# Two-layer attention encoder on one core: source order kept longer, returned outputs split a step ahead, more early subtractions on GpSimd

## The chip, the cores and the metric

The kernel runs on one core of a Trainium2 chip. A core has a matrix engine (TensorE, PE in the profile; its weight loads are listed as PEld), a vector engine (VectorE, DVE), a scalar engine (ScalarE, ACT), a general engine (GpSimd, POOL) and a queue engine that issues most transfers (SyncE, SP). Each engine works through its own list of instructions in order and waits at an instruction until what it needs is there. The metric is the device time of one execution in microseconds.

## The reference

Input x has 512 tokens of width 1024, in float32. Two layers follow one another, each with the same frame: RMS norm, one projection to queries, keys, values and a gate, attention with RMS-normed queries and keys, output times silu(gate), output projection, residual add.

```python
def mixer_a(hn, w_in, w_out, q_gain, k_gain, t5_bias):      # layer A
    qkv = proj[..., :n_qkv].reshape(b, s, N_DIL_GROUPS, 3, N_HEADS, HEAD_DIM)
    for g, (window, dilation) in enumerate(((128, 1), (512, 4), (2048, 16))):
        q = rms_norm(qkv[:, :, g, 0], q_gain[g]); k = rms_norm(qkv[:, :, g, 1], k_gain[g])
        o, lse = dilated_group_attention(q, k, qkv[:, :, g, 2], ..., dilation, reach)
        ...
    y = jnp.sum(softmax(lses)[..., None] * outs, axis=0) * jax.nn.silu(gate)
    return y @ w_out
```

Layer A is dilated sliding-window attention with three dilations (1, 4, 16), 16 heads each, merged by their softmax denominators. Layer B is neighbourhood attention on an 8 x 64 grid with 16 heads.

## The kernel before

**Products.** All products are in float32 accuracy made of three passes in a faster format: a weight block `wraw` is cast to `wh` on ACT (`cast`, line 157), the rest `wl = wraw - wh` is subtracted on DVE or POOL (`rest`, line 162), and PE multiplies high by high, high by low and low by high (`mm3`). A job is one 512 (or 384) columns wide block of weights: one cast, one subtraction, then its matmuls. `splits` (line 292) makes the jobs four to five ahead of PE, and chooses the engine of each subtraction by a fraction `pool[0] = [a, b]`: a of b subtractions go to POOL.

**Layer A.** The heads are taken in eight pairs (`hc` = 0 to 7). `main_a` is PE's main work for a pair: the projections. For pairs 1 to 7 it uses a scheme with seven block products in place of eight, on sums of weight blocks and on sums `mixed` of halves of the normed input. These four sums are made once, in `mix` (line 525), and split into `mix_h` (cast on ACT) and `mix_l` (subtracted on POOL or DVE). `gate_a` projects the gate, `v0_a` the values of the first dilation. `attn_a` works on the pair before, woven into the projections: `q_a` and `k_a` transpose queries and keys on PE into PSUM banks (`tp`) and copy them out (`k0h`, `k0l`, `q0h`, `q0l`, `q12`, `k12`), `scores` makes logits (`log`), `minima`, `exponents` and `normalise` make the softmax, the probabilities are transposed into `pt`, and `weigh` makes the products with v (`o`). `head_norm` scales raw queries and keys (`rawq`, `rawk`) by the inverse root `rs` of their sums of squares `ss`; the root is a chain of eleven tiny DVE instructions on `nv`, `na` and `rs`. Four PSUM banks hold accumulators (`acc`), four hold everything else.

**Between the layers.** The outputs of pairs 0 to 5 go to DRAM (`y_d`). At the end of layer A `y_back` brings them back into a tile `yr`, and `y_split` splits each into `y_h` (ACT) and `y_l` (DVE for odd pairs, POOL for even ones). Pair 6 is split straight from its tile `gt`. `out_product` then runs the output projection over `y_h` and `y_l`, first four output blocks for pair 0, then pair 1 and so on, while the attention of pair 7 is woven in; the products with pair 7 come last.

**What sets the order.** PE's list is the order of the source, in which `run` weaves the attention and all timed calls (`later_on`) into the projections by a clock that counts PE's own work. The lists of the other engines are made by a scheduler, which may move an instruction, unless it is marked: while `held[0]` is true every instruction of DVE, ACT, POOL and SP that is written through `vec`, `act`, `pol` and `syn` is kept in the order of the source. `main` sets `held[0] = hc > 0` at the start of each pair, and `project_qk`'s `normed` sets it false once the keys of pair 7 are scaled.

Of the kernel before, what the change touches and what calls it, by code (L numbers as in the profile page):

```python
# [13 lines left out]
F32 = mybir.dt.float32  # L14
# [8 lines left out]
P = 128  # L23
S = 512
D = 1024
DH = 64
NHC = 8
# [19 lines left out]
def tile_hybrid_encoder(  # L47
# [244 lines left out]
    def splits():  # L292
        casts, queue, due = [], [], plan.loads(lead)
        for at, (raw, c, step, n) in enumerate(plan.jobs):
            pool[0] = [0, 1] if at < start_jobs + 16 else [1, 2] if at < mixed_jobs else [2, 5]
            for r in due.get(at, ()):
                load(r)
            for add in plan.sums.get(at, ()):
                add()
            casts.append((cast(raw.tile[:, c : c + step], step), n))  # L300
            if len(casts) > 1:
                done, m = casts.pop(0)
                queue.append((*rest(*done), m))
            if len(queue) > 4:
                yield queue.pop(0)
        done, m = casts.pop(0)
        queue.append((*rest(*done), m))
        yield from queue
# [216 lines left out]
    def mix():  # L525


        x11, x12, x21, x22 = (x_all[:, k : k + KH, t : t + H] for t in (0, H) for k in (0, KH))
        t = wk.tile([P, 2, KH, H], F32, tag="tr", name="mixed", bufs=1)
        a, b = t[:, 0], t[:, 1]  # L530

        def put(n, out, op, x, y, eng):
            with in_order():
                op(out, x, y)
                act.copy(mix_h[:, n], out)
                eng.tensor_sub(mix_l[:, n], out, mix_h[:, n].bitcast(F32))
            stamp["mix", n] = 0

        yield "wait", ("first",), 500
        yield from first_out()  # L540
        yield 1500
        put(0, a, vec.tensor_sub, x21, x22, pol)
        yield 2000
        put(1, b, vec.tensor_sub, a, x11, vec)
        yield 2000
        yield from bias_lines()
        yield "wait", ("rawk", 0), 1000
        put(3, b, vec.tensor_add, b, x12, pol)
        yield 5000
        put(2, a, vec.tensor_sub, x11, x21, vec)  # L550

    def row_sums(ssq):

# [38 lines left out]
    st = {}  # L592
# [19 lines left out]
    def project_qk(n, ns, key, hc, guard, first=False, **kw):  # L612
# [3 lines left out]
        def evac(i, acc):  # L616
            if not box:
                box.append(raw_q() if key == "rawq" else part(0) if key == "rawk" else raw_b(hc, n))
                box.append(sums())
            raw, ss = box  # L620
            dst, src = raw[:, i, :], acc[:, :n]
            if first:
                act.copy(dst, src)
                return
            act.activation(dst, src, AF.Copy, scale=rs_n[:, i : i + 1])
            (squares_soon if key != "raw" else squares)(raw[:, i, : ns * 64], ss, i, ns, key != "raw")
# [10 lines left out]
    def normed(raw, ss, ns, key, hc):  # L637

        def go():
            with in_order() if hc == 0 and key != "raw" else nullcontext():  # L640
                head_norm(raw, ss, ns, key == "raw")
            st[key, hc] = raw
            stamp[key, hc] = clock[0]
            if (key, hc) == ("rawk", NHC - 1):
                held[0] = False

        if (key, hc) == ("rawk", 0):
            later_on(4000, go)
# [24 lines left out]
    def v0_a(hc, guard=None):  # L673
        acc = []
        yield from project_t(acc)
        yield guard
        home = "q12" if hc < NHC - 1 else "tr"
        vt = wk.tile([P, 1024], F32, tag=home, name="vt", bufs=1)
        act.copy(by_place(vt[:, 64:EXT]), by_class(acc[0]))
        act.copy(vt[:, 0:64], vt[:, EXT - 64 : EXT])  # L680
        st["vt", hc] = vt
# [177 lines left out]
        return gt  # L859

    def y_back(hcs, tag):
        t = wk.tile([P, 4, S], F32, tag=tag, name="yr", bufs=1)
        syn.dma_start(t[:, : len(hcs), :], y_d[:, hcs[0] : hcs[-1] + 1, :])
        return t

    def y_split(t, hc):
        src = t.rearrange("p (t ja x) -> p x ja t", t=4, ja=8)
# [70 lines left out]
    def attn_a(hc):  # L938
# [122 lines left out]

        if last:
            rows = []
            for u in range(2):
                room = part(0)
                mine = [
                    (tile_[:2], *minima(*tile_, room[:, n, :] if u else None)) for n, tile_ in enumerate(scores(u))
                ]
                for _, _, row, mn in mine:
                    exponents(row, mn)  # L1070
                    normalise(row, mn)
                rows += mine
                yield 4000
            for (hd, t), pr, _, _ in rows:
                turn_p(hd, t, pr)
                yield 700
            yield from v_a(hc)
            yield "wait", ("gate", hc), 500
            gt = weighed(hc, (yield from weigh()))
            stamp["ya", "turned"] = 0  # L1080
            for c in range(4):
                src = gt.rearrange("p (t ja x) -> p x ja t", t=4, ja=8)[:, 4 * c : 4 * c + 4]
# [33 lines left out]
        if hc < NHC - 2:  # L1116
# [7 lines left out]
                yield 1500  # L1124
                yield from q_a(hc + 1)
            return
        back = y_back(range(4), "tr")
        stamp["back",] = 0
        yield "wait", ("rawk", hc + 1), 0
        for n in range(2):  # L1130
            y_split(back[:, n, :], n)
        for n in (2, 3):
            later_on(3000 + 2000 * n, partial(y_split, back[:, n, :], n))
        yield from q_a(hc + 1)
        more = y_back(range(4, NHC - 2), "rawq")
        for n in range(4, NHC - 2):
            later_on(2000 * n - 3000, partial(y_split, more[:, n - 4, :], n))
        later_on(9000, partial(y_split, gt, hc))

    pending = []  # L1140

# [378 lines left out]
```

## Time and profile before

| | |
|---|---|
| median of the runs | 864.33 us (861.68 to 864.4) |
| the profiled execution | 865.5 us, of which the span of instructions is 863.7 us |
| PE busy | 838.7 us (97%) |
| DVE, ACT, POOL busy | 630.8, 509.1, 288.7 us |
| mean granted PE clock | 0.988 of full speed |
| subtractions `wl` | 207 on DVE, 153 on POOL |

Layer A's projections run from about 2 to 523 us, its output projection to about 600 us, layer B to the end. The figures in the profile are microseconds from the start of the span unless marked ns; a bracket at the end of a row of the timeline is how long the engine sat idle before the row, and what ended the wait. In tables by stretch, PEclk is the clock granted to PE (1.00 is full speed).

### The profile page before, as it was taken

The page shows a single profiled execution, that of the slowest core. Times are in us where ns is not written, and L with a number is a line of the kernel's source. Part 1 is how long each engine was busy: PE and PEld are TensorE (multiplying, and loading weights), DVE is VectorE, ACT ScalarE, POOL GpSimd, SP SyncE. Part 2 cuts the span into 40 slices and gives each one's busy share as a digit, 9 for nine tenths or more (in the row PEclk, how much of TensorE's full clock was granted, in tenths as well). Part 3 has the DMA queues.
Part 4 walks back from the last instruction along what each step waited for, and adds up shares of the span by engine and source line. Part 5 has one row for each costly group of instructions (what it writes and reads, how often), then busy time and mean ns, then how long its engine had stood idle before and what let it go on. Part 6 is the DMA issues. An engine that isn't in the chain of part 4 may idle for free. (4 is left out here: it accounts for less than half of the span.)

```text
span 863.7 us, 18127 instructions
## 1 busy us (share of the span) xinstructions
PE 838.7 (97%) x6611; PEld 693.6 (80%) x6611; DVE 630.8 (73%) x1655; ACT 509.1 (59%) x1066; POOL 288.7 (33%) x257
## 2 busy tenths in 40 slices
PE   9989988999999999999999998999999999999998
PEld 6867767878877878878878876889998898889776
DVE  6889894787887787887787866547577667866742
ACT  7565763674765855946846828545366645665440
POOL 5041531363462452442543513111223223322301
PEclk9999998999999999999999998999999999999999
DMA  9424755567667765775776662284264456545212
GB/s 341 131 62 125 192 125 146 107 164 216 128 164 216 147 165 176 153 181 166 162 172 182 137 217 104 74 275 139 93 173 143 125 166 184 162 129 139 83 50 98
DMA packets 56169, 131.97 MB, mean 153 GB/s; under 512 B 7184, under 2 KB 24528, under 8 KB 55952
## 3 DMA queue, kind: packets, MB, share of 16 engines
q1 hardware_dynamic: 49744, 108.78, 40.8%
q0 software_dynamic: 6048, 22.02, 15.0%
q8 instruction: 52, 0.85, 0.4%
q14 instruction: 37, 0.30, 0.1%
q10 hardware_dynamic: 288, 0.01, 0.0%
HBM read 111.73 MB, written 11.72 MB: 143 GB/s over the span
## 5 line engine op out<-in xcount | busy, mean ns | idle before, releaser
L85 POOL TENSOR_TENSOR wl<-wraw,wh 128x512 fp32r<-128x512 f32 (+1 forms) x153 | 197.8, 1294 | 448.5 <-PE acc L323 227.8
L85 ACT CAST wh<-wraw 128x512 fp32r<-128x512 f32 (+1 forms) x360 | 209.9, 593 | 194.3 <-PE acc L323 152.7
L85 DVE TENSOR_TENSOR wl<-wraw,wh 128x512 fp32r<-128x512 f32 (+1 forms) x207 | 160.4, 779 | 49.3 <-PE acc L323 34.5
L323 PE MATMUL acc<-wh,hn_h 128*128 128x384 f32 (+1 forms) x488 | 186.7, 382 | 3.1 <-DVE gt L85 1.8
L323 PE MATMUL acc<-wl,hn_h 128*128 128x384 f32 (+1 forms) x488 | 178.2, 365 | 2.7 <-DVE wl L85 2.7
L323 PE MATMUL acc<-wh,hn_l 128*128 128x384 f32 (+1 forms) x488 | 178.0, 365 | 0.0
L85 ACT ACTIVATE p<-p,mn 128x256 f32<-128x256 f32 (+2 forms) x248 | 137.8, 584 | 33.8 <-DVE mn L85 33.8
L323 PEld LDWEIGHTS acc<-wh,hn_h 128*128 128x128 f32 x488 | 92.5, 189 | 21.8 <-issue 6.6
L323 PEld LDWEIGHTS acc<-wl,hn_h 128*128 128x128 f32 x488 | 92.8, 190 | 11.2 <-DVE wl L85 3.7
L323 PEld LDWEIGHTS acc<-wh,hn_l 128*128 128x128 f32 x488 | 92.4, 189 | 9.9
L323 PE MATMUL acc<-wl,mix_h 128*128 128x512 f32 x224 | 87.4, 390 | 1.9 <-DVE wl L85 1.5
L323 PE MATMUL acc<-wh,mix_h 128*128 128x512 f32 x224 | 89.1, 398 | 0.0
L323 PE MATMUL acc<-wh,mix_l 128*128 128x512 f32 x224 | 87.4, 390 | 0.0
L323 PE MATMUL acc<-hn_h,wh 128*128 128x512 f32 x192 | 79.3, 413 | 0.3 <-ACT rawb L85 0.2
L323 PE MATMUL acc<-hn_h,wl 128*128 128x512 f32 x192 | 75.7, 394 | 3.1 <-DVE wl L85 3.1
L323 PE MATMUL acc<-hn_l,wh 128*128 128x512 f32 x192 | 75.7, 394 | 0.0
L85 DVE STREAM_TRANSPOSE pt<-p 128x512 f32<-128x512 f32 (+1 forms) x60 | 40.6, 688 | 23.8 <-ACT p L85 23.6
L85 DVE TENSOR_REDUCE ss<-sq 128x4 f32<-128x256 f32 (+1 forms) x96 | 46.3, 502 | 13.6 <-ACT sq L85 6.8
L323 PE MATMUL acc<-y_h,wh 128*128 128x512 f32 x128 | 52.6, 411 | 2.5 <-ACT gt L85 1.9
L323 PEld LDWEIGHTS acc<-wl,mix_h 128*128 128x128 f32 x224 | 42.1, 188 | 11.0 <-DVE wl L85 2.0
L323 PE MATMUL acc<-y_l,wh 128*128 128x512 f32 x128 | 50.4, 394 | 0.0
L323 PE MATMUL acc<-y_h,wl 128*128 128x512 f32 x128 | 50.3, 393 | 0.0
(145 smaller groups left out, 1364.1 us busy)
## 6 DMA issues: line engine op xcount, KB each, us to landing
wraw<-in_w SPq DMA_DIRECT2D x95, 512.0 KB
wraw<-in_w POOLq DMA_DIRECT2D x42, 512.0 KB, 7.0
wraw<-in_w SPq DMA_DIRECT2D x38, 384.0 KB
pt<-pt SPq DMA_DIRECT2D x112, 64.0 KB
td<-tr SPq DMA_DIRECT2D x24, 224.0 KB
pt<-td SPq DMA_DIRECT2D x24, 224.0 KB
e<-l_d SPq DMA_DIRECT2D x32, 112.0 KB
e<-l_d SPq DMA_DIRECT2D x16, 128.0 KB
```

Source lines behind the costliest of these rows:

```text
L85: m = f(*args, **kw)
L323: nc.tensor.matmul(o, l, r, **kw)
```

## The change

Five edits. (1) `held[0]` becomes true when the first keys of pair 0 are taken out of PSUM, earlier than before, and stays true until the last products with v (`weigh` of pair 7) are written. Where the last pair's softmax was a plain list of instructions, it now comes by timed calls, as that of the other pairs. (2) The `mix_l` of the mixed sum n = 2, the last of the four to be made, goes from DVE to POOL. (3) For the 24 jobs that follow the first 32, two of three subtractions go to POOL, where it was one of two: 16 instead of 12. (4) `y_back` brings pairs 0 and 1 first and then pairs 2 to 5 in one transfer, where it was 0 to 3 and then 4 and 5; the split of pair n is called at 1000 + 2500 n of the clock after the second transfer's call, that of pair 6 at 16000. (5) The last pair's `vt` (raw values) is put into the free half of the first `yr` tile, where it had to wait for a tile that held returned outputs.

```diff
@@ splits
-            pool[0] = [0, 1] if at < start_jobs + 16 else [1, 2] if at < mixed_jobs else [2, 5]
+            first = at - start_jobs
+            pool[0] = [0, 1] if first < 16 else [2, 3] if first < 40 else [1, 2] if at < mixed_jobs else [2, 5]
@@ mix
-        put(2, a, vec.tensor_sub, x11, x21, vec)
+        put(2, a, vec.tensor_sub, x11, x21, pol)
@@ project_qk
+                held[0] = held[0] or (key == "rawk" and hc == 0)
...
-            if (key, hc) == ("rawk", NHC - 1):
-                held[0] = False
@@ v0_a
-        home = "q12" if hc < NHC - 1 else "tr"
-        vt = wk.tile([P, 1024], F32, tag=home, name="vt", bufs=1)
+        vt = st["tail"][:, 1024:] if hc == NHC - 1 else wk.tile([P, 1024], F32, tag="q12", name="vt", bufs=1)
@@ y_back
-        t = wk.tile([P, 4, S], F32, tag=tag, name="yr", bufs=1)
-        syn.dma_start(t[:, : len(hcs), :], y_d[:, hcs[0] : hcs[-1] + 1, :])
-        return t
+        t = wk.tile([P, 4 * S], F32, tag=tag, name="yr", bufs=1)
+        y = t[:, : len(hcs) * S].rearrange("p (n s) -> p n s", n=len(hcs))
+        syn.dma_start(y, y_d[:, hcs[0] : hcs[-1] + 1, :])
+        return t, y
@@ attn_a, last pair
+            def soft(n, tile_, room):
+                pr, row, mn = minima(*tile_, room)
+                rows.append((*tile_[:2], pr))
+                later_on(1500, partial(exponents, row, mn))
+                later_on(2900, partial(normalise, row, mn))
+
             for u in range(2):
                 room = part(0)
-                mine = [
-                    (tile_[:2], *minima(*tile_, room[:, n, :] if u else None)) for n, tile_ in enumerate(scores(u))
-                ]
-                for _, _, row, mn in mine:
-                    exponents(row, mn)
-                    normalise(row, mn)
-                rows += mine
-                yield 4000
-            for (hd, t), pr, _, _ in rows:
-                turn_p(hd, t, pr)
+                for n, tile_ in enumerate(scores(u)):
+                    later_on(400 + 900 * n, partial(soft, n, tile_, room[:, n, :] if u else None))
+                yield 5000
+            for n in range(8):
+                turn_p(*rows[n])
                 yield 700
             yield from v_a(hc)
             yield "wait", ("gate", hc), 500
             gt = weighed(hc, (yield from weigh()))
+            held[0] = False
@@ attn_a, pair 6
-        back = y_back(range(4), "tr")
+        st["tail"], back = y_back(range(2), "tr")
...
-        for n in (2, 3):
-            later_on(3000 + 2000 * n, partial(y_split, back[:, n, :], n))
         yield from q_a(hc + 1)
-        more = y_back(range(4, NHC - 2), "rawq")
-        for n in range(4, NHC - 2):
-            later_on(2000 * n - 3000, partial(y_split, more[:, n - 4, :], n))
-        later_on(9000, partial(y_split, gt, hc))
+        _, more = y_back(range(2, NHC - 2), "rawq")
+        for n in range(2, NHC - 2):
+            later_on(1000 + 2500 * n, partial(y_split, more[:, n - 2, :], n))
+        later_on(16000, partial(y_split, gt, hc))
```

Most lists stay as they were. PE's own list is the same up to the first logits of the last pair. The other lists differ at three places. In the rows below, the number behind a name counts tiles; the same tile can have another number in the two kernels.

DVE at the end of the first keys' projection (pair 0) and the start of pair 1, before; `wl_617` belongs to the first half of gate 0:

```order
L85 TENSOR_TENSOR hn_l_93<-pt_98,hn_h_92 128x512
L85 TENSOR_TENSOR mix_l_95<-mixed_401,mix_h_94 128x1024
L85 TENSOR_REDUCE ss_582<-sq_584 128x4
L85 TENSOR_REDUCE ss_582<-sq_591 128x4
L85 TENSOR_REDUCE ss_582<-sq_598 128x4
L85 TENSOR_REDUCE ss_582<-sq_605 128x4
L85 TENSOR_TENSOR wl_617<-wraw_251,wh_575 128x512
L85 TENSOR_TENSOR wl_627<-wraw_251,wh_615 128x512
L85 TENSOR_TENSOR wl_637<-wraw_290,wh_625 128x512
L85 TENSOR_TENSOR wl_647<-wraw_290,wh_635 128x512
```

The same place now:

```order
L85 TENSOR_TENSOR hn_l_93<-pt_98,hn_h_92 128x512
L85 TENSOR_TENSOR wl_609<-wraw_251,wh_575 128x512
L85 TENSOR_TENSOR mix_l_95<-mixed_401,mix_h_94 128x1024
L85 TENSOR_REDUCE ss_582<-sq_592 128x4
L85 TENSOR_REDUCE ss_582<-sq_598 128x4
L85 TENSOR_TENSOR wl_625<-wraw_251,wh_607 128x512
L85 TENSOR_REDUCE ss_582<-sq_614 128x4
L85 TENSOR_REDUCE ss_582<-sq_620 128x4
L85 TENSOR_TENSOR wl_637<-wraw_290,wh_623 128x512
L85 TENSOR_TENSOR wl_647<-wraw_290,wh_635 128x512
```

The subtraction for the first half of the gate moved ahead of the split `mix_l` and of the four sums of squares, that for the second half between these sums.

DVE further on, at the mixed sum n = 2 and the first pair's `k0l`, before:

```order
L85 TENSOR_TENSOR wl_725<-wraw_143,wh_699 128x512
L85 TENSOR_TENSOR mixed_401<-pt_98 128x1024
L85 TENSOR_TENSOR mix_l_95<-mixed_401,mix_h_94 128x1024
L85 SCALAR_TENSOR_TENSOR gt_715<-eg_716,gt_715 128x256
L85 TENSOR_TENSOR wl_758<-wraw_143,wh_723 128x512
L85 SCALAR_TENSOR_TENSOR k0l_744<-tp_746,gk_155,k0h_743 128x512
L85 SCALAR_TENSOR_TENSOR gt_715<-eg_716,gt_715 128x256
L85 TENSOR_TENSOR wl_776<-wraw_195,wh_756 128x512
```

The same place now:

```order
L85 TENSOR_TENSOR wl_725<-wraw_143,wh_699 128x512
L85 TENSOR_TENSOR mixed_401<-pt_98 128x1024
L85 SCALAR_TENSOR_TENSOR gt_715<-eg_716,gt_715 128x256
L85 TENSOR_TENSOR wl_758<-wraw_143,wh_723 128x512
L85 SCALAR_TENSOR_TENSOR k0l_744<-tp_746,gk_155,k0h_743 128x512
L85 SCALAR_TENSOR_TENSOR gt_715<-eg_716,gt_715 128x256
L85 TENSOR_TENSOR wl_776<-wraw_195,wh_756 128x512
```

The `mix_l` left DVE, and everything behind it moved up by one; on POOL it stands right behind the `mix_l` of the sum n = 3, and so ahead of a weight transfer that POOL issues next.

ACT at the end of layer A, from the first copy of pair 7's queries and keys, before:

```order
L85 ACTIVATE k0h_6376<-tp_6379,gk_155 128x512
L85 CAST wh_6398<-wraw_6125 128x512
L85 CAST q0h_6374<-tp_6405 128x512
L85 CAST wh_6429<-wraw_6153 128x512
L85 COPY q12_6378<-tp_6421 128x512
L85 CAST y_h_6245<-yr_6317 128x512
L85 COPY q12_6378<-tp_6439 128x512
L85 CAST y_h_6245<-yr_6317 128x512
L85 CAST wh_6473<-wraw_6153 128x512
L85 ACTIVATE gt_6462<-acc_6395 128x512
L85 ACTIVATE k12_6455<-tp_6456,gk_155 128x512
L85 COPY vt_6392<-acc_6322 128x4x4x32
```

The same place now:

```order
L85 ACTIVATE k0h_6376<-tp_6379,gk_155 128x512
L85 COPY yr_6317<-acc_6322 128x4x4x32
L85 COPY yr_6317<-yr_6317 128x64
L85 CAST wh_6397<-wraw_6125 128x512
L85 CAST q0h_6374<-tp_6404 128x512
L85 COPY q12_6378<-tp_6420 128x512
L85 CAST wh_6426<-wraw_6153 128x512
L85 COPY q12_6378<-tp_6436 128x512
L85 ACTIVATE k12_6450<-tp_6451,gk_155 128x512
L85 ACTIVATE gt_6457<-acc_6394 128x512
L85 ACTIVATE eg_6458<-gt_6457 128x512
L85 CAST wh_6468<-wraw_6153 128x512
```

The copy of `vt` out of its accumulator moved from the twelfth row to the second, the two casts `y_h` left, and the copy `k12`, which waits for a transpose on PE, now stands ahead of the gate's copy `gt`.

DVE just ahead of this place, before:

```order
L85 TENSOR_TENSOR rawk_160<-rawk_160,rs_6336 128x256 x4
L85 TENSOR_TENSOR wl_6364<-wraw_6101,wh_6325 128x512
L85 TENSOR_TENSOR y_l_6246<-yr_6317,y_h_6245 128x512
L85 SCALAR_TENSOR_TENSOR k0l_6377<-tp_6379,gk_155,k0h_6376 128x512
L85 TENSOR_TENSOR wl_6400<-wraw_6125,wh_6362 128x512
```

The same place now:

```order
L85 TENSOR_TENSOR rawk_160<-rawk_160,rs_6336 128x256
L85 TENSOR_TENSOR y_l_6246<-yr_6317,y_h_6245 128x512
L85 TENSOR_TENSOR rawk_160<-rawk_160,rs_6336 128x256
L85 TENSOR_TENSOR wl_6364<-wraw_6101,wh_6325 128x512
L85 TENSOR_TENSOR rawk_160<-rawk_160,rs_6336 128x256 x2
L85 SCALAR_TENSOR_TENSOR k0l_6377<-tp_6379,gk_155,k0h_6376 128x512
L85 TENSOR_TENSOR wl_6399<-wraw_6125,wh_6362 128x512
```

The split `y_l` of pair 1 moved ahead of three of the four scalings of the last keys and of a weight subtraction. Behind these rows, ACT's list now has the cast `y_h` of pair 2 ahead of the first softmax exponent of pair 7, and those of pairs 3 to 6 between the exponents.

## The prediction

> **What bounds the kernel now.** I read the engines' busy times first, then the waits of PE, then PE's timeline at the waits, then a table by stretches for the clock. Their rows, from the page of the profile and from PE's timeline:
>
> ```profile
> PE 838.7 (97%) x6611; PEld 693.6 (80%) x6611; DVE 630.8 (73%) x1655; ACT 509.1 (59%) x1066; POOL 288.7 (33%) x257
> ...
> 65.21 0.50 PE L323 MATMUL acc<-hn_h,wl 128*128 128x512 f32 x1 [3.07 <-DVE wl L85]
> 82.52 0.50 PE L323 MATMUL acc<-wl,mix_h 128*128 128x512 f32 x1 [1.52 <-DVE wl L85]
> 123.80 0.80 PE L323 MATMUL acc<-wl,hn_h 128*128 128x512 f32 x1 [2.34 <-DVE wl L85]
> 134.24 0.69 PE L323 MATMUL o<-pt,rawk 32*64 32x128 f32 x4 [1.83 <-DVE k0l L85]
> 524.46 0.66 PE L327 MATMUL tp<-ident,rawk 128*128 128x128 f32 x4 [1.16 <-DVE k0l L85]
> 528.92 0.50 PE L323 MATMUL acc<-y_h,wh 128*128 128x512 f32 x1 [1.86 <-ACT gt L85]
> 530.46 0.80 PE L323 MATMUL acc<-y_h,wh 128*128 128x512 f32 x1 [0.57 <-ACT vt L85]
> ```
>
> PE is busy 97% of the span, so only 25 us of idle time (863.7 less 838.7) and what a lowered clock costs can be won. The seven rows are the waits over half a microsecond that the change touches or stands beside; their brackets add up to 12.35 us. They lie in two places. The first four are in the first two pairs of heads, where PE waits for DVE: for subtractions `wl`, and for `k0l`, which must free a PSUM bank. The last three are at the end of layer A, where PE waits for `k0l` again and for ACT to empty the accumulators of the gate and of the last values. Between these places the lists of all engines are as before, and behind the last products with v nearly so.
>
> The stretches on both sides of these waits (us; PE, PEld, DVE, ACT and POOL busy, then PEclk, DMA share, GB/s):
>
> ```profile
> 62.20:65.60 3.40, 0.39 (x2) 0.35 (x3) 2.07 (x5) 3.39 (x8) 0.52 (x1) 1.00 0.56 87
> 65.60:69.00 3.40, 3.40 (x10) 2.66 (x9) 3.06 (x14) 0.00 (x0) 0.00 (x0) 0.50 0.58 117
> 79.20:82.70 3.50, 1.98 (x11) 1.33 (x11) 2.40 (x4) 3.48 (x6) 0.00 (x0) 1.00 0.69 133
> 120.20:123.60 3.40, 1.26 (x6) 0.71 (x4) 3.33 (x7) 0.93 (x2) 0.00 (x0) 1.00 0.39 96
> 123.60:127.00 3.40, 3.20 (x8) 2.53 (x9) 3.40 (x6) 1.45 (x3) 2.41 (x3) 0.50 0.53 92
> 130.40:133.90 3.50, 1.66 (x16) 0.94 (x14) 3.32 (x10) 2.04 (x4) 0.68 (x1) 0.99 0.70 142
> 133.90:140.70 6.80, 6.22 (x156) 5.49 (x158) 1.55 (x4) 0.00 (x0) 0.00 (x0) 0.50 0.51 148
> 526.40:529.80 3.40, 1.54 (x8) 0.90 (x7) 1.64 (x2) 3.40 (x6) 1.55 (x1) 1.00 0.63 205
> 529.80:536.60 6.80, 6.23 (x83) 4.60 (x83) 2.22 (x12) 5.07 (x10) 2.79 (x2) 0.50 0.21 80
> ```
>
> Each wait that leaves PE busy for less than half of a stretch of 3.4 us is followed by one or two such stretches at a PEclk of 0.50: behind 0.39, 1.26, 1.66 and 1.54 us of work. The wait at 82.52, with 1.98 of 3.5 us busy, is not. So the clock prices a wait here: 3.4 us at half speed lose 1.7 us, 6.8 us lose up to 3.4.
>
> [...]
>
> **Part 1, the first gate (order of the source).** Rows of ACT, DVE, POOL and PE around it:
>
> ```profile
> 53.89 0.61 ACT L85 CAST wh<-wraw 128x512 fp32r<-128x512 f32 x1
> ...
> 60.30 0.41 DVE L85 TENSOR_REDUCE ss<-sq 128x4 f32<-128x256 f32 x1
> 64.48 2.49 DVE L85 TENSOR_TENSOR wl<-wraw,wh 128x512 fp32r<-128x512 f32 x4
> 74.11 3.34 DVE L85 TENSOR_TENSOR wraw<-wraw 128x1024 f32<-128x1024 f32 x1
> 80.31 1.23 DVE L85 TENSOR_TENSOR mix_l<-mixed,mix_h 128x1024 fp32r<-128x1024 f32 x1 [1.11 <-ACT mix_h L85]
> 81.78 0.68 DVE L85 TENSOR_TENSOR wl<-wraw,wh 128x512 fp32r<-128x512 f32 x1
> ...
> 73.98 2.39 POOL L85 TENSOR_TENSOR mix_l<-mixed,mix_h 128x1024 fp32r<-128x1024 f32 x1 [11.26 <-ACT mix_h L85]
> ...
> 78.78 0.40 PE L323 MATMUL acc<-wh,mix_h 128*128 128x512 f32 x1
> ```
>
> Before, the subtraction for the first half of gate 0 stands behind `mix_l` (59.17, just ahead of these rows) and four sums of squares, and runs first of the four at 64.48. Its input was cast at 53.89. DVE waits in between for ACT's squares: from 60.71 to 64.48 it does three sums of about 0.42, so 2.5 us are idle. Now this subtraction stands ahead of `mix_l`, and is done at about 59.8, before PE asks at 62.0. The one for the second half waits for its cast and for POOL's `hn_l` until about 63.2, and PE asks at 64.7. So the wait of 3.07 and the half-speed stretch behind it (1.7) go: PE is 4.8 ahead, and reaches the first mixed product (78.78) at 74.0.
>
> What is late next is DVE itself. It has the same work, but 1.8 of its 2.5 idle us are used, so the rest of its list comes 1.8 earlier, not 4.8. Its addition at 74.11 takes 3.34, because POOL's `mix_l` holds it until 76.37; that collision stays. The subtraction behind it comes at 78.06 less 1.8 = 76.2, and PE asks at 74.25: a new wait of 2.0.
>
> **Part 2, `mix_l` of n = 2 to POOL.** On DVE it cost a wait of 1.11 and 1.23 of work ahead of the subtraction at 81.78, and PE its 1.52 at 82.52. Now that wait is 0.25. But POOL needs 2.39 for what DVE did in 1.23, and it runs beside the subtraction of the next job, which has two inputs in SBUF and is held as the addition was: I take 1.0 there (between 0, if DVE comes first, and 2.4).
>
> Parts 1 and 2: 3.07 + 1.7 + 1.52 - 2.0 - 0.25 - 1.0 = 3.0 us, from -1 (the held subtraction costs 2.4, and the wait of 2.0 lowers the clock once) to 5 (no hold).
>
> **Part 3, four more subtractions on POOL.** Rows of DVE and POOL:
>
> ```profile
> 104.31 1.28 DVE L85 TENSOR_TENSOR rawq<-rawq,acc 128x512 f32<-128x512 f32 x2
> 118.21 0.19 DVE L85 TENSOR_TENSOR na<-rs 128x32 f32<-128x32 f32 x1
> 118.43 1.27 DVE L85 SCALAR_TENSOR_TENSOR na<-na,nv 128x32 f32<-128x32 f32 x1
> ...
> 103.31 1.36 POOL L85 TENSOR_TENSOR wl<-wraw,wh 128x512 fp32r<-128x512 f32 x1 [0.36 <-PE acc L323]
> 118.36 1.30 POOL L85 TENSOR_TENSOR wl<-wraw,wh 128x512 fp32r<-128x512 f32 x1 [1.91 <-ACT wh L85]
> ```
>
> A subtraction takes 1.30 on POOL. A DVE instruction with both inputs in SBUF that meets one is held: the root's step took 1.27 at 118.43 instead of 0.19 (118.21). With one input in PSUM it isn't: the two at 104.31 took 0.64 each beside POOL's 103.31. DVE gives up net three subtractions (2.0 us) between 90 and 117. But the root at 117 hangs on ACT's squares and softmax rows, which don't move, so I see it start 0.4 earlier, and POOL's subtraction at 118.36 still falls into it. The subtraction on which PE waits 2.34 at 123.80 stands behind this root and its scalings, and moves by 0.3. Behind it POOL has one subtraction more, beside the second root: 0.2 to 0.5 later for `k0l` at 134.24. I take 0 for both waits together, between -3 (two more holds of 1.3 in the root) and +2 (the root clears POOL, and 1.08 of hold and part of the wait go). PE's list isn't touched, and these waits keep their half-speed stretches.
>
> POOL's weight transfer behind the moved `mix_l` is issued at about 81 now. Its block of 512 KB is used by the product after the take-outs at 104.31; even 10 us (what 1 MB took from 510.33 to 520.13, rows below) land it before. I cost it at nothing.
>
> **Part 4, the end of layer A.** Rows of the queue, ACT, DVE and PE:
>
> ```profile
> 510.33 0.33 SPq L85 DMA_DIRECT2D yr<-y_d  x1
> ...
> 520.13 2.10 ACT L85 CAST y_h<-yr 128x512 fp32r<-128x512 f32 x2 [3.86 <-DMA yr<-y_d]
> 528.26 0.61 ACT L85 ACTIVATE gt<-acc 128x512 f32<-128x512 f32 x1
> 529.32 1.09 ACT L85 COPY vt<-acc 128x512 f32<-128x512 f32 x1
> 537.21 1.27 ACT L85 ACTIVATE p<-p,mn 128x448 f32<-128x448 f32 x2
> 544.14 0.72 ACT L85 ACTIVATE rawk<-rawk,mn 128x512 f32<-128x512 f32 x1 [1.59 <-DVE mn L85]
> ...
> 522.26 1.49 DVE L85 TENSOR_TENSOR y_l<-yr,y_h 128x512 fp32r<-128x512 f32 x1 [1.51 <-ACT y_h L85]
> 549.12 0.39 DVE L85 COPY pt<-tp 128x256 f32<-128x256 f32 x1
> ...
> 535.50 0.79 PE L323 MATMUL acc<-y_h,wh 128*128 128x512 f32 x1
> 557.18 2.71 PE L323 MATMUL o<-pt,rawk 32*64 32x128 f32 x128
> ```
>
> ACT waits 3.86 for the first returned outputs, until 520.13. That transfer is now half as large (512 KB less, and the weights behind it wait for the second transfer), of 9.8 us from issue to landing: I take 1.5 to 2 us earlier. The two casts (2.10) are done at about 520.4, not 522.2. DVE's `y_l` (1.49) now stands ahead of three scalings and a subtraction, 1.6 us in all, so `k0l` comes within 0.5 of before, and the wait at 524.46 stays. From 520.4 ACT does a weight cast and `k0h` (1.1), the two copies of the last values (1.09 and 0.3, done at 522.8, where it was 530.4), five copies and casts (2.9), `k12` and at 526.2 the gate (528.26 before). So the waits of 1.86 and 0.57 go but for 0.1, PE is never under half busy, and the 6.8 us at half speed go. From 524.5 PE runs two transposes (0.4 each), six matmuls behind each (1.4 each) and the logits (3.5 at half speed ahead of 535.50, so about 2): its row of 535.50 comes at about 530.3. That is 5.2, and 0.6 more for the half speed that lasts until 536.6.
>
> Against it: ACT does the casts of pairs 2 to 6 in the order of the source, four of them between the exponents. The second transfer is issued at about 522, when the tile of the raw queries is free, and asked for at 529: the gate's end at 526.7, four instructions of 0.5 to 0.7. I take 6 us to landing, 528. From the first minima (531.2), ACT has eight exponents of 0.8 (0.72 and the reading of the sum), five scalings of 0.63, four casts of 1.06 and three of weights of 0.42 until the eighth exponent ends: 15.0, 546.2. DVE waits there for it, and then has seven transposes and six copies of about 0.4 (549.12), a subtraction of 0.5 and a wait of 0.5 for its cast: 552.4. PE's work from 535.50 to 557.18 took 21.7, 0.6 of it for the clock, so it asks for them at 530.3 + 21.1 = 551.4: a wait of 1.0. The split of pair 6 ends 0.4 after PE asks. Part 4 gives 5.8 - 1.4 = 4.4, from 1 (the first rival) to 6.
>
> **Sum.** 3.0 + 0 + 4.4 = 7.4 us. The profiled execution took 865.5, so 858.1; the median of the runs is 1.2 lower (864.33), so I forecast 857.
>
> **Rivals.**
> - *Part 4 fails by the first transfer.* If it lands as late as before, `y_l` ahead of the scalings makes `k0l` 1.7 later, PE waits 2.9 and the half-speed stretches stay: part 4 gives 1, in all 4, so 860.4. For it: other transfers share the time; against: 512 KB less.
> - *Part 1 and 2 fail.* DVE stays the limit until 85 and holds eat the 3.0: 859.9.
> - *POOL holds DVE throughout.* Four subtractions and a `mix_l` are 7.6 us on POOL, and spare DVE 4.0. If every one holds DVE in a stretch that PE waits for, that is 3.6 lost (1.0 is counted), and a pair of half-speed stretches more (3.4): 858.1 + 6 less 1.2, about 863, no change. Against: most of DVE's work there has an input in PSUM.
> - *The clock doesn't follow the waits.* Then only idle time counts: 1.3 in parts 1 and 2, 1.0 in part 4, 2.3 in all: 862. [...]
> - *Slower: the second transfer is late.* In the source's order all of ACT's softmax of pair 7 stands behind the cast that needs it. From a landing at 529 on, each us of lateness is one of PE, and over 1.7 us PE falls to half speed for 6.8 us (3.4). With that, 4.0 us of lateness eat the 3.0 + 4.4, and 4.0 + 2.6 = 6.6 make a clear loss: a landing at 535.6, nearly 14 us after the issue, where 1 MB took 9.8 beside weights. From there on 867 and more.
>
> **How the numbers follow.** From no change this kernel can be told by about 0.3% (2.6 us). My forecast (854 to 861.5) has 0.48, part 4 failing alone 0.14, parts 1 and 2 failing alone 0.12, POOL's holds 0.10, the clock 0.03, slower 0.13 (the late transfer, and waits that I don't see in a list that can no longer be rearranged). Faster is thus 0.74, same 0.13, slower 0.13. The range takes in the best of all parts nearly whole (864.33 less 13 is 851.3) and goes up to the border of no change: 851.5 to 864.5.
>
> **What would show it.** Right: no wait of PE near 62, a new one of about 2 us at the first mixed product; the wait at 123 us nearly as before; no half-speed stretch at the end of layer A, ACT's copy of the values straight behind `k0h`, and a short wait at the last products with v. Wrong: PEclk at 0.50 behind `k0l` of pair 7, ACT waiting long for the second transfer, or DVE's root at 117 stretched by several holds.

## The result

Over 12 runs each, the changed kernel took 862.23 us and the kernel before 863.57 us (medians): a ratio of 0.999, with an interval of 0.997 to 1.001. Twelve more runs of the unchanged files gave 0.9988 (0.9975 to 1.0001). So the change gives about 1 us, which is no clear difference, where 7.4 were forecast. The profiled execution took 864.2 us (span 862.5); the prediction's sum for it was 858.1.

Busy times and PE's waits after, from the page and from PE's timeline:

```profile
PE 833.5 (97%) x6611; PEld 689.0 (80%) x6611; DVE 634.5 (74%) x1650; ACT 508.2 (59%) x1066; POOL 295.6 (34%) x262
...
76.20 0.50 PE L324 MATMUL acc<-wl,mix_h 128*128 128x512 f32 x1 [1.86 <-DVE wl L85]
79.88 0.63 PE L328 MATMUL tp<-ident,rawk 128*128 128x128 f32 x4 [0.87 <-DVE k0l L85]
120.62 0.50 PE L324 MATMUL acc<-wl,hn_h 128*128 128x512 f32 x1 [1.55 <-DVE wl L85]
131.84 0.69 PE L324 MATMUL o<-pt,rawk 32*64 32x128 f32 x4 [4.07 <-DVE k0l L85]
523.96 0.66 PE L328 MATMUL tp<-ident,rawk 128*128 128x128 f32 x4 [1.66 <-DVE k0l L85]
541.50 0.50 PE L324 MATMUL acc<-y_l,wh 128*128 128x512 f32 x1 [0.82 <-POOL y_l L85]
549.10 0.50 PE L324 MATMUL acc<-y_l,wh 128*128 128x512 f32 x1 [1.11 <-POOL y_l L85]
553.17 0.66 PE L328 MATMUL tp<-ident,yr 128*128 128x128 f32 x4 [0.17 <-DVE pt L85]
554.27 0.40 PE L324 MATMUL o<-pt,rawk 32*64 32x128 f32 x2 [0.44 <-DVE pt L85]
554.84 2.09 PE L324 MATMUL o<-pt,rawk 32*64 32x128 f32 x113 [0.17 <-DVE pt L85]
558.18 0.47 PE L324 MATMUL o<-pt,rawk 32*64 32x128 f32 x13 [1.26 <-issue]
```

The waits for gate 0 (3.07 before) and for the last gate and values (1.86 and 0.57) are gone, as meant. In their place stand a new wait of 0.87 for a `k0l` of pair 0, one of 4.07 for that at 132 us, which was 1.83, and a row of new ones behind the last gate, 3.97 us together. The stretches (us; PE, PEld, DVE, ACT and POOL busy, then PEclk, DMA share, GB/s):

```profile
62.00:65.40 3.40, 3.40 (x16) 2.82 (x16) 3.33 (x8) 3.40 (x8) 1.46 (x2) 1.00 0.29 28
127.30:130.70 3.40, 0.43 (x4) 0.19 (x4) 3.15 (x10) 0.50 (x1) 0.95 (x1) 1.00 0.74 158
130.70:137.50 6.80, 5.42 (x141) 4.69 (x143) 2.35 (x6) 0.00 (x0) 0.00 (x0) 0.50 0.53 140
526.00:529.40 3.40, 3.40 (x77) 2.72 (x81) 1.44 (x4) 3.31 (x6) 1.28 (x1) 1.00 0.57 213
```

PE is busy throughout at gate 0 and at the last gate, and the half-speed stretches there are gone. The one behind `k0l` is as long as before.

PE's list is nearly the same in all kernels here, so the same product can be found in each trace and the time between two of them compared. This table does it for all profiled executions (us; the heads are the times in the kernel before, and the end is the start of the last product):

| kernel | 20 to 140 | 140 to 523 | 523 to 541 | 541 to 559 | 559 to end |
|---|---|---|---|---|---|
| before | 120.6 | 382.4 | 18.1 | 18.4 | 299.9 |
| before, once more (E5) | 120.6 | 382.9 | 16.5 | 18.4 | 299.8 |
| changed | 118.1 | 384.0 | 12.8 | 23.5 | 299.8 |
| changed, once more (E6) | 117.3 | 383.8 | 12.5 | 23.3 | 299.8 |
| parts 1 to 3 alone (E1) | 117.6 | 382.6 | 17.5 | 18.4 | 299.7 |
| part 4 alone (E2) | 120.6 | 384.5 | 12.7 | 22.0 | 299.7 |
| without part 3 (E3) | 117.9 | 382.9 | 12.6 | 22.0 | 299.8 |
| earlier splits (E4) | 118.5 | 384.2 | 12.8 | 21.6 | 299.7 |
| later root (E7) | 110.6 | 383.3 | 12.3 | 22.0 | 299.9 |
| later root and more (E8) | 110.5 | 384.6 | 12.7 | 22.1 | 299.7 |
| before, later root (E9) | 115.2 | 382.8 | 16.0 | 18.4 | 299.7 |
| parts 1 to 3, later root (E10) | 110.6 | 384.6 | 17.9 | 18.4 | 299.9 |
| without part 3, later root (E11) | 113.3 | 382.8 | 12.0 | 23.0 | 299.8 |
| later root, two splits earlier (E12) | 110.6 | 383.3 | 13.0 | 19.5 | 299.8 |

The third and fourth column of numbers tell the fate of part 4: it wins 5.3 us up to the first logits of pair 7 and gives 5.1 back before the last products with v are done.

### The profile page after: what moved, and what is told of

Its sections match the earlier page's. It is cut to its first block, busy times and chain, and to the rows that moved or that the text cites. A ratio compares the mean times of both kernels' runs of the same rounds, so it can differ in the third digit from the quotient of the medians.

```text
span 862.5 us, 18120 instructions
## 1 busy us (share of the span) xinstructions
PE 833.5 (97%) x6611; PEld 689.0 (80%) x6611; DVE 634.5 (74%) x1650; ACT 508.2 (59%) x1066; POOL 295.6 (34%) x262
## 4 chain that ended last, share of the span: by engine, by line
PE 69%; DVE 10%; ACT 9%; DMA 5%; issue 5%; POOL 1%; ACTq 0%; DVEq 0%; POOLq 0%; SPq 0%
PE acc L324 57%; ACT p L85 5%; PE o L324 5%; PE log L324 4%; DMA wraw<-in_w 4%; PE tp L328 2%; DVE na L85 2%; DVE wl L85 2%; ACT wh L85 2%; ACT rawk L85 1%; DMA yr<-y_d 1%; DVE p L85 1%; DVE rawq L85 1%; DVE rawk L85 1%; DVE gt L85 1%
## 5 line engine op out<-in xcount | busy, mean ns | idle before, releaser
L85 POOL TENSOR_TENSOR wl<-wraw,wh 128x512 fp32r<-128x512 f32 (+1 forms) x157 | 202.3, 1297 | 432.7 <-PE acc L324 216.7
L85 DVE TENSOR_REDUCE ss<-sq 128x4 f32<-128x256 f32 (+1 forms) x96 | 46.3, 502 | 12.5 <-POOL sq L85 6.2
L324 PEld LDWEIGHTS acc<-wl,mix_h 128*128 128x128 f32 x224 | 42.1, 188 | 12.8 <-DVE wl L85 3.5
## 6 DMA issues: line engine op xcount, KB each, us to landing
wraw<-in_w SPq DMA_DIRECT2D x38, 384.0 KB
```

The costliest lines, as they stand in the source:

```text
L85: m = f(*args, **kw)
L324: nc.tensor.matmul(o, l, r, **kw)
```

## The experiments

All ratios are to runs of the kernel before on the same chip.

**E1, parts 1 to 3 alone.** The three edits of `splits`, `mix` and `project_qk`'s start put into the kernel before:

```diff
-            pool[0] = [0, 1] if at < start_jobs + 16 else [1, 2] if at < mixed_jobs else [2, 5]
+            first = at - start_jobs
+            pool[0] = [0, 1] if first < 16 else [2, 3] if first < 40 else [1, 2] if at < mixed_jobs else [2, 5]
-        put(2, a, vec.tensor_sub, x11, x21, vec)
+        put(2, a, vec.tensor_sub, x11, x21, pol)
+                held[0] = held[0] or (key == "rawk" and hc == 0)
```

> Parts 1 to 3 alone, the end of layer A as before. If what PE wins in the first two pairs stays won (as the prediction summed it), PE is 2 to 3 us ahead at 140 us and still at 524 us, and the time is 2 to 3 us less than before (0.997). If the weight transfers between pairs set a floor (the changed kernel lost 0.55 us at 340 and 0.5 us at 465 at products that wait for ACT, whose cast ahead waits for a weight block), PE is 2 to 3 us ahead at 140, at most 1.7 at 342, about 1.1 at 466 and about 0.5 at 524, and the time is 0 to 1 us less.

Measured: 862.33 us, 0.9978 (0.9966 to 0.999), so 1.9 us less. PE was 3.3 us ahead at 140 us and 3.0 at 523: the lead was kept, and the floor set by weight transfers fell.

**E2, part 4 alone.** The changed kernel with those three edits taken back.

> Part 4 alone, the first two pairs as before. By the prediction's term it is worth 4.4 us (0.995). If the lists of ACT, DVE and POOL behind the gate give back what the gate won (the changed kernel lost about 5 us between 541 and 560 us: 0.8 and 1.1 at the splits of pairs 4 and 6, 0.8 at the last probabilities, 1.3 inside the products with v), PE is 5 to 6 us ahead at the first logits of pair 7 and about 0.7 us behind these products, and the time is 0 to 1.5 us less. If the weight transfers ate the front's gain, PE's lead stays within 0.2 us of zero from 140 to 523 us here.

Measured: 865.15 us, 1.0008 (0.9993 to 1.0024): worth nothing, where 4.4 us were forecast. In the table its 523 to 541 us are 5.4 shorter, its 541 to 559 us 3.6 longer. Between 140 and 523 us, where its lists are those of before, it lost 2.2 us. That isn't shown to come from its edits: the column goes from 382.4 to 384.6 and follows no part (E10, without part 4, has 384.6, and E3, with it, 382.9). About half of the 2.2 us is idle time of PE, most of it at waits for ACT's `k` near 280 us (0.71 in the kernel before, 0.82 and 0.72 here); why these differ stays open.

**E3, without the four more subtractions on POOL.** The changed kernel with the old line for `pool[0]`.

> Everything but the four more subtractions on POOL. If three POOL subtractions in a row held DVE's root for 4.4 us at 124 us, that step takes 0.2 to 1.6 us here, PE's wait for k0l falls from 4.1 to under 2 us, and the wait for a subtraction at 120 us grows to about 2.3. By the prediction (this part is worth nothing) PE's lead at 140 us is as in the changed kernel, 2.7 us, within 1. The time: as the changed kernel's within 0.5 us if the weight transfers cut any lead down to 1.7 us at 341; else it moves by what the lead at 140 moves.

Measured: 863.4 us, 0.9988 (0.997 to 1.0006), the changed kernel's own ratio. The wait at 121 us was 2.36 and that for `k0l` 1.61, each followed by one stretch of 3.4 us at half speed; PE's lead at 140 us was 2.9, where the changed kernel's was 2.7. So the four subtractions move a wait and win nothing there. Without them two steps of the root behind this `k0l` are held, for 1.28 and 1.14 us (1.28 and 1.22 in the kernel before), each beside one subtraction on POOL. What makes `k0l` late in the changed kernel stands in DVE's and POOL's timelines of it:

```profile
123.72 0.17 DVE L85 TENSOR_TENSOR na<-rs 128x16 f32<-128x16 f32 x1
123.93 4.37 DVE L85 SCALAR_TENSOR_TENSOR na<-na,nv 128x16 f32<-128x16 f32 x1
128.33 0.18 DVE L85 SCALAR_TENSOR_TENSOR rs<-na,rs 128x16 f32<-128x16 f32 x1
...
131.04 0.74 DVE L85 SCALAR_TENSOR_TENSOR k0l<-tp,gk,k0h 128x512 fp32r<-128x512 f32 x1
...
124.22 4.03 POOL L85 TENSOR_TENSOR wl<-wraw,wh 128x512 fp32r<-128x512 f32 x3
```

One tiny step of the root, 0.17 us elsewhere, took 4.37: its row begins just ahead of three subtractions that POOL ran back to back, and it ended as the last of them did (128.25). In E6 it took 4.35 beside 4.03 on POOL.

**E4, earlier splits.** The changed kernel with

```diff
-            later_on(1000 + 2500 * n, partial(y_split, more[:, n - 2, :], n))
-        later_on(16000, partial(y_split, gt, hc))
+            later_on(500 + 1500 * n, partial(y_split, more[:, n - 2, :], n))
+        later_on(9500, partial(y_split, gt, hc))
```

> The changed kernel with the splits of pairs 2 to 5 called at 500 + 1500 n and that of pair 6 at 9500 of the clock (1000 + 2500 n and 16000). The returned outputs had landed at 525.6 us in the changed kernel, 2.6 us ahead of the first cast that needs them. If the place of the casts between the exponents in ACT's list is what makes PE wait, its waits for y_l of pairs 4 and 6 (0.8 and 1.1) go, DVE's minima come earlier and the waits for the last probabilities (0.8) go too: 2 to 3 us less than the changed kernel, 859.5 to 860. If ACT and DVE simply have too much work for the time between 528 and 555 us, the waits move to the first logits or to the last probabilities and the time stays at 862.

Measured: 861.13 us, 0.9965 (0.9949 to 0.9981), about 2 us less than the changed kernel's ratio gives. Both waits for `y_l` are gone; those for the last probabilities stayed (0.78), a new one for a minimum (0.54) came, and PE stopped again inside the products with v. The place of the casts in ACT's list is the cause of the first two. In the changed kernel:

```profile
537.53 1.27 ACT L85 ACTIVATE p<-p,mn 128x448 f32<-128x448 f32 x2
538.70 1.11 ACT L85 CAST y_h<-yr 128x512 fp32r<-128x512 f32 x1
...
545.02 1.34 ACT L85 ACTIVATE rawk<-rawk,mn 128x512 f32<-128x512 f32 x2 [1.36 <-DVE mn L85]
546.26 0.19 ACT L85 ACTIVATION_READ_ACCUMULATOR rawk<-rawk,mn 128x1 f32 x1
546.35 1.08 ACT L85 CAST y_h<-gt 128x512 fp32r<-128x512 f32 x1
...
539.89 1.55 POOL L85 TENSOR_TENSOR y_l<-yr,y_h 128x512 fp32r<-128x512 f32 x1 [8.90 <-ACT y_h L85]
...
547.51 1.53 POOL L85 TENSOR_TENSOR y_l<-gt,y_h 128x512 fp32r<-128x512 f32 x1 [5.10 <-ACT y_h L85]
```

No cast waits for its data. Each stands behind exponents, one pair of them behind a wait of 1.36 us for DVE's minima, and POOL, idle for 8.9 and 5.1 us, then needs 1.5 us for what PE already waits for.

**E5, the kernel before, profiled once more.**

> The kernel before, unchanged, profiled once more. The prediction took its half-speed stretches (65.6 to 69.0, 123.6 to 127.0, 133.9 to 140.7 and 529.8 to 536.6 us, together 20.5 us, 10.2 us lost) and its small waits between 140 and 524 us as fixed. If they are fixed, this profile shows the same stretches behind the same waits within half a microsecond and the same starts of the products within 0.5 us. If the stretches hang on where a wait falls against the clock's own windows of 3.41 us, some are gone or are half as long, at waits of the same length; and the waits for ACT between 140 and 524 us (0.42 at 178, 0.71 at 279 and none over 0.2 later) have other lengths, up to 2 us in all.

Measured: 864.33 us. The three waits of the first 140 us and their half-speed stretches came again (65.4, 123.4 and 133.7 us, 17 and 3 times 3.41 us apart). At the end of layer A there was one such stretch, not two:

```profile
529.60:533.00 3.40, 3.40 (x8) 1.94 (x10) 1.03 (x3) 3.23 (x7) 0.00 (x0) 0.50 0.23 92
533.00:536.40 3.40, 3.40 (x83) 2.81 (x84) 1.90 (x11) 2.84 (x6) 2.81 (x2) 1.00 0.28 59
```

It was one in E1 and E9 too, two in E10 and in the profile of the prediction. The 34 runs of the kernel before beside E1 to E4 show granted clocks from 0.986 to 0.994, 0.991 in the mean: 7.9 us lost, where the profiled execution (0.988 of 863.7) lost 10.4.

**E6, the changed kernel, profiled once more.**

> The changed kernel, unchanged, profiled once more. If the hole of 1.26 us inside the products with v at 558 us belongs to the order of the lists, it is there again. If it is a late fetch of PE's instructions (a 16 KB packet of an instruction queue began at 555.8 us there, and 4 us or more ahead of these products in the executions without a hole), it is there only when that packet starts less than 3 us ahead of the stop. The hold of DVE's root by three POOL subtractions (4.4 us) and the waits at the splits of pairs 4 and 6 (0.8 and 1.1) come from the lists and are there again, within 0.2. Time 0.998 to 0.999 of before.

Measured: 863.19 us, 0.9988. The hold and the waits for `y_l` came again within 0.02 us. So did the stop in the products with v (0.98 us). In the trace's packets, the 16 KB packet of a queue of kind instruction (q8) began at 554.69 us and PE went on at 557.13. Over all 14 profiled executions such a packet stands near these products. PE stops in five (the changed kernel, E4, E6, E8, E11), each time behind 114 or 115 of the 128 products, and there the packet began after the first product, 2.3 to 2.6 us before PE went on; in the other nine it began 1.5 to 4.2 us ahead of the first product, and there is no stop. All five have the new end of layer A; of the nine, four have. That PE stopped for the instructions in this packet is a reading that fits; no row shows what it waited for (its bracket says issue), and what makes the packet late isn't settled.

**E7, a later root.** The changed kernel; the root for the keys of pair 1 is written 3.2 us of the clock later (the transposes of those keys stay where they were):

```diff
-            later_on(2200, go)
+            later_on(5400 if (key, hc) == ("rawk", 1) else 2200, go)
-        yield "wait", ("rawk", hc), 9000 if 1 < hc < NHC - 1 else 12000 if hc < 2 else 8000
+        yield "wait", ("rawk", hc), 9000 if 1 < hc < NHC - 1 else 12000 if hc < 1 else 8800 if hc < 2 else 8000
```

> The changed kernel with the root for the keys of pair 1 written 3.2 us of the clock later, so that k0l and q0l stand ahead of it in DVE's list; POOL's list is the same. If the hold of the root by POOL is what PE's wait of 4.1 us at 132 us consists of, that wait falls under 0.5 us although the root may be held as before, the half-speed stretch behind it (6.8 us) goes, PE is 3.5 to 7 us further ahead at 141 us, and the time is 3 to 5 us less than the changed kernel's. If DVE as a whole is too late there, the wait moves to the products with v of pair 0 or to the first product of pair 2 and the time falls by less than 1 us. If the waits for ACT between 140 and 524 us eat what comes early, PE's further lead shrinks below 2 us by 524 us.

Measured: 854.98 us, 0.989 (0.9871 to 0.9909), more than expected. DVE, POOL and PE:

```profile
124.69 0.75 DVE L85 SCALAR_TENSOR_TENSOR k0l<-tp,gk,k0h 128x512 fp32r<-128x512 f32 x1 [0.54 <-ACT k0h L85]
126.41 0.69 DVE L85 TENSOR_TENSOR q0l<-tp,q0h 128x512 fp32r<-128x512 f32 x1 [0.97 <-ACT q0h L85]
127.02 1.32 DVE L85 TENSOR_SCALAR nv<-ss 128x16 f32<-128x16 f32 x1
...
124.25 4.04 POOL L85 TENSOR_TENSOR wl<-wraw,wh 128x512 fp32r<-128x512 f32 x3
...
126.55 2.83 PE L324 MATMUL o<-pt,rawk 32*64 32x128 f32 x128
```

POOL's three subtractions are where they were, `k0l` and `q0l`, each with one input in PSUM, run beside them in 0.75 and 0.69 us (0.74 to 0.75 and 0.68 to 0.69 in the kernel before and the changed one), and only the root, which nobody waits for now, meets their end. The 128 products run without a stop, and no stretch of this execution is at half speed before its end (its mean granted clock is 1.0): the 7.5 us that the first column of the table lost are the wait of 4.07 and half of the 6.8 us at half speed behind it.

**E8, all together.** E7 with the splits of E4, and `y_l` of pair 1 written behind `k0l` and `q0l` of pair 7 (a third argument of `y_split` delays its subtraction alone):

```diff
-            y_split(back[:, n, :], n)
+            y_split(back[:, n, :], n, 6000 * n)
```

> Together: the earlier splits, the later root, and at pair 7 the subtraction y_l of pair 1 written behind k0l and q0l instead of ahead of them. If each cause stands for itself: no wait for k0l at 522 us (1.7 to 2.2 in the changed kernel and in the front alone), 3 to 5 us from the root, 1 to 2.5 from the splits: 855 to 858 us, 0.990 to 0.993 of before. If what comes early is eaten by waits for ACT or for the transfers, 859 to 861.

Measured: 854.81 us, 0.9884 (0.9866 to 0.9901): no better than E7. The wait for `k0l` at pair 7 (1.2 in E7) and those for `y_l` went, but waits of 0.49 for the gate's copy and of 0.83 for a minimum came. This profile also has the stop in the products with v (1.16 us), which E7's has not, and 1.3 us more between 140 and 523 us, with a wait of 1.1 for ACT's keys. So it isn't shown whether splits that stand ahead of the minima and exponents win time or only pass the lateness on.

**E9, the later root alone**, in the kernel before.

> The kernel before with nothing but the later root for the keys of pair 1 (k0l and q0l ahead of it in DVE's list). If the wait for k0l and the half-speed stretches behind it are one separate loss, before's 1.8 us at 134 us and the 6.8 us at half speed behind it go: 1.8 + 0.3 + 3.4 = 5.5 us less, 0.9935 to 0.995 of before, while the waits at 65, 82 and 124 us stay. If the later root only pays together with the four subtractions on POOL (since these made the wait long), it is worth under 2 us here.

Measured: 859.39 us, 0.9943 (0.992 to 0.9965): 4.9 us less. The loss behind the root is one of its own, and was there before the change.

**E10, parts 1 to 3 and the later root**, with the old end of layer A.

> Parts 1 to 3 and the later root, the end of layer A as before. If part 4 is worth nothing (alone it measured 1.0008 of before), the time is that of the kernel with all parts and the later root, 855 us within 0.7. If part 4 is worth what its profile shows from 524 us on (332.5 us without the hole against 332.9 to 334.8 with the old end), it is 0.4 to 2 us longer here. If part 4 costs 1.3 us between 141 and 524 us (382.4 to 382.9 us in the profiles without it, 382.9 to 384.6 with it), that stretch takes 382.3 to 383 us here.

Measured: 856.67 us, 0.99 (0.9876 to 0.9924). Its interval and E7's overlap: part 4 as it stands is worth about 1 us, if anything. The waits of 1.87 and 0.57 for the gate and the values are back, with two half-speed stretches.

**E11, without part 3, but with the later root.**

> All parts and the later root, but 12 of the 24 subtractions on POOL as before. By the prediction the four more subtractions are worth nothing: 855 us here too. If they only moved their gain into the wait for k0l, which the later root removes, they are worth here what they save at 121 us: a wait of 2.4 instead of 1.5 us and up to 3.4 us at half speed behind it, 1 to 3 us more, 856 to 858.

Measured: 858.91 us, 0.9937 (0.9915 to 0.9958), against 0.989 with the four subtractions on POOL. By these ratios they are worth about 4 us once nothing behind them takes it back. The profiles show 2.7 of it in the first 140 us (113.3 against 110.6); 1.0 more is the stop in the products with v, which E11's has and E7's has not:

```profile
122.03 0.50 PE L323 MATMUL acc<-wl,hn_h 128*128 128x512 f32 x1 [2.36 <-DVE wl L85]
```

This wait (1.54 in E7) has a half-speed stretch behind it here (123.4 to 126.9 us), and not in E7.

**E12, two splits earlier.** E7 with only the splits of pairs 4 and 6 moved:

```diff
-            later_on(1000 + 2500 * n, partial(y_split, more[:, n - 2, :], n))
-        later_on(16000, partial(y_split, gt, hc))
+            later_on(9500 if n == 4 else 1000 + 2500 * n, partial(y_split, more[:, n - 2, :], n))
+        later_on(14000, partial(y_split, gt, hc))
```

> All parts and the later root, and only the splits of pair 4 (9500 of the clock, was 11000) and pair 6 (14000, was 16000) earlier, which moves the cast of each ahead of one or two exponents in ACT's list and nothing in DVE's. If the two waits for y_l (0.86 and 1.12 us, each with 0.3 to 0.4 us behind it until PE is back in step) are separate losses, they go: 2 to 2.6 us less, about 852.7. If ACT's list is full there, the waits move to the exponents and from there to the last probabilities, as with all splits earlier: 854.5 to 855.5.

Measured: 853.2 us, 0.9871 (0.9847 to 0.9895), the fastest kernel here, by its ratio 11 us less than before, though its interval overlaps E7's. POOL's two splits:

```profile
531.04 1.58 POOL L85 TENSOR_TENSOR y_l<-yr,y_h 128x512 fp32r<-128x512 f32 x1 [7.08 <-ACT y_h L85]
536.67 1.58 POOL L85 TENSOR_TENSOR y_l<-gt,y_h 128x512 fp32r<-128x512 f32 x1 [4.05 <-ACT y_h L85]
```

PE has no wait for them, and its 541 to 559 us took 19.5 instead of 22.0 us. These 2.6 us (before rounding) are the two waits of 0.86 and 1.12 and 0.3 us more for each. So the loss was in the place of two casts, and ACT had room for them.

## Why the prediction was wrong

- **Parts 1 and 2 (3.0 us): the steps right, the sum too high at first.** The wait at gate 0 and its half-speed stretch went (PE was 5.0 us further ahead, forecast 4.8), and the new wait at the first mixed product came at 76.20 with 1.86 us (forecast 76.2 and 2.0). But at 100 us PE had won 1.8 us since 20 us in every kernel with these parts, not 3.0: behind 76 us it waited 0.87 for `k0l`, 0.33 for a subtraction and 1.01 for ACT's `k` (0.47 before). E3, without part 3, has won 2.7 us by 140 us, as one stretch at half speed stands behind its `k0l` and not two; parts 1 to 3 together (E1) measured 1.9 us (0.9 to 2.9).
- **Part 3 (0 us): right in sum, wrong in its places.** Both waits were said to stay. The one at 124 us fell to 1.55 and lost its half-speed stretch; the one for `k0l` grew by 2.2 us. The step that failed is the hold: one subtraction more beside this root was to make `k0l` 0.2 to 0.5 us later, but where single subtractions had held two steps for 1.2 to 1.3 us each, three in a row held one step for 4.4 us. That the two cancel here is chance; E11 shows what part 3 wins without the second.
- **Part 4, what it wins (5.8 us): right for the profile it was made from.** The product that stood at 535.50 came at 529.8 (forecast 530.3), and the gate's waits and half-speed stretches went; the second transfer was early, not late (its last packet ended at 525.6 us, forecast 528). But 1.7 of this is the second half-speed stretch, which only some executions of the kernel before have.
- **Part 4, "against it" (1.4 us): this is the term that failed.** It measured 5.1 us: 0.82 and 1.11 for the splits of pairs 4 and 6 and 0.6 behind them, 0.78 for the last probabilities (forecast 1.0), 1.5 for the stop in the products with v, and 0.3 in small pieces. The sum had ACT work through its list from the first minima without a pause. In fact ACT and DVE wait for each other in their fixed lists (1.36 us at 545.02), so that the casts came later than added up. The split of pair 6 was in the sum, with 0.4 of its 1.1 us; that of pair 4 was put at nothing without a reason. E12 shows that the place of their two casts made both waits. The stop in the products with v was no step of the sum, and what makes it come stays open; without it (E2) the term is 3.6 us.
- **The one profiled execution.** The sum of idle time (2.3 of 7.4 us) and of clock (5.1) was made against an execution that had lost 2.5 us more to the clock than the kernel's mean, and 140 to 523 us that happened to be the shortest of all fourteen. In the changed kernel's 12 runs the clock costs 5.1 us in the mean, 2.8 less than the 7.9 of the kernel before, where the sum had 5.1 less.
- **Against the profiled execution** 6.1 us are missing: 3.7 in "against it", 1.6 between 140 and 523 us, 0.5 at the first 140 us, 0.5 at `k0l` of pair 7, which leaves 0.2 too much.
- **The rivals.** *POOL holds DVE throughout* gave the right time, and its mechanism was at work at one place, for 4.4 us; but what part 3 saved paid for it, so it isn't what made the result. *The clock doesn't follow the waits* gave 862 as well and is wrong: with the waits gone, E7 runs at 1.00 until its last product. *Parts 1 and 2 fail* came true in part: PE had 1.8 and not 3.0 us at 100 us, after two waits for DVE. The first transfer's lateness and the second's did not occur.

## What to carry to other kernels

Where an instruction that another engine waits for stands behind a chain that nobody waits for yet, in an in-order list, change the order of the two before making either engine faster: this one reordering gave 5 us alone and 8 us on top of the change, whose five edits together gave 1. When work is moved to an engine whose instructions hold another's, look for where it will run back to back: here three in a row held one tiny step for 4.4 us, though another row let the other engine in. And a saving in half-speed time, read from one execution, needs the clocks of many runs before it goes into a sum.

## What the runs showed of the hardware

- A DVE instruction with two inputs in SBUF was held through three POOL instructions (4.37 us beside 4.03), and not let in between them. Another row of subtractions on POOL did not hold it so. In the changed kernel, further on:

```profile
176.93 6.66 POOL L85 TENSOR_TENSOR wl<-wraw,wh 128x512 fp32r<-128x512 f32 x4 [0.98 <-ACT wh L85]
...
178.25 2.38 DVE L85 TENSOR_TENSOR wl<-wraw,wh 128x512 fp32r<-128x512 f32 x2
181.75 0.68 DVE L85 TENSOR_TENSOR wl<-wraw,wh 128x512 fp32r<-128x512 f32 x1
```

  Here DVE's subtractions, also with two inputs in SBUF, got in between: the second took 1.66 and ended 2.9 us ahead of POOL's row, and the third took 0.68. In the row at 124.22 each subtraction begins about 0.3 us before the one ahead of it ends, in this one 0.04 before it or behind it (0.14 us for the second); whether that decides is open. Nor did an earlier start let DVE through at 123.93: its row begins 0.29 us ahead of POOL's first subtraction (though behind the start of a transfer's issue on POOL at 123.61), and yet it was held.
- The same wait at the same product lowered the clock in one execution and not in another. Ten profiles have a wait of 1.86 to 1.89 us at 76 to 77 us. In eight of them, the changed kernel's among them (1.00), the second product `acc<-wh,mix_l` behind it took 0.39 to 0.40 us; in E4 and E6 it took 0.63, at half speed. E6's wait, in PE's timeline:

```profile
76.86 0.50 PE L324 MATMUL acc<-wl,mix_h 128*128 128x512 f32 x1 [1.88 <-DVE wl L85]
```

  and the stretches behind it and at the wait for `k0l`:

```profile
78.20:81.60 3.40, 3.21 (x11) 2.19 (x10) 2.64 (x4) 3.40 (x7) 2.50 (x2) 0.50 0.42 145
126.00:129.40 3.40, 2.08 (x20) 1.36 (x17) 3.30 (x4) 2.08 (x4) 2.89 (x3) 0.99 1.04 223
129.40:136.20 6.80, 3.48 (x108) 3.08 (x116) 4.15 (x12) 0.00 (x0) 0.00 (x0) 0.50 0.51 135
```

  The half-speed stretches start at 65.59, 123.62, 133.86 and 529.80 us in the kernel before (17, 20 and 136 times 3.41 us behind the first), at 7.84, 130.72 and 861.17 in the changed one (36 and 250 times), and E6's two are 15 times 3.41 us apart: whole multiples within each of the three, but at other times than in the next one. The stretch of E6 at 78.20 cost nothing in the end: the waits behind it were shorter (0.19 for `k0l` instead of 0.87), and at 100 us PE had won the same 1.8 us as in the others. So the waits behind this stretch took its loss up.
- Half speed did not go by busy time alone: in the second of these rows PE is busy for 2.08 of 3.4 us, more than half, much of it with transposes and products of a 32 by 64 tile, and 0.50 follows. What is counted stays open.
- PE stopped for 0.7 to 1.3 us in 5 of 14 executions, at the same place, behind 114 or 115 of 128 products. In these five a 16 KB packet of the instruction queue q8 began 2.3 to 2.6 us before PE went on, behind the first product; in the other nine it began 1.5 to 4.2 us ahead of the first product. That PE stopped for this packet is a reading that fits, not a row.
